# 192 of 512 tokens gather their expert rows instead of 128, and 64 of the dense tokens carry both weight parts in one stationary tile

## The chip, the cores and the metric

The kernel runs on one core of one Trainium2 chip. The metric is the device time of one execution in microseconds (us). The core has five engines: TensorE (PE in the profile, with its weight loads as PEld), VectorE (DVE), ScalarE (ACT), GpSimd (POOL) and SyncE (SP). 16 DMA engines move data; transfers are issued by SP, ACT and POOL.

## The reference, cut to what matters

One decoder layer over 512 tokens of width 1024. A mixing half (projections, a short convolution, a gated recurrence, an output projection) is followed by a feed-forward half that selects experts, and a last norm. The change touches the feed-forward half only:

```python
q = (xt @ wq).reshape(t, 8, 2, 128)                       # 8 heads, two halves
scores = einsum('thpd,hpnd->thpn', q, keys)               # 128 keys per half
s_top, i_top = lax.top_k(scores, 16)
cand = s_top[:, :, 0, :, None] + s_top[:, :, 1, None, :]  # 16 x 16 pairs
c_score, c_idx = lax.top_k(cand, 16)
expert = i1 * 128 + i2                                    # 1 of 16384
gates = softmax(c_score)
u = take(u_tab, expert); a = gelu(einsum('td,thkd->thk', x, u))
vv = take(v_tab, expert); y = einsum('thk,thkd->td', gates * a, vv)
```

So each token has 8 x 16 = 128 experts; an expert is one row of 1024 float32 (4096 bytes) in a table of u and one in a table of v.

## The kernel before, in words

**Two ways to the same sum.** Block 0 (tokens 0 to 127, one token a partition) gathers: for each of its 128 expert slots one indirect DMA of POOL brings a row of u per partition (`gu`, line 675), DVE multiplies it with the normed token and sums (line 677); later another brings the row of v (`gv`, line 683) and DVE adds it with its weight to `y0` (line 685). The other 384 tokens (`TD`) are dense: all 16384 experts are multiplied out, in 128 chunks of 128 experts, with the gates as a matrix that is zero where an expert wasn't chosen.

**Precision.** A dense product is made of three matmuls (`mm3`, lines 112 to 115): both factors are split in a high and a low part (`whi`, `wlo`, `wh`, `wl`), and high*high, low*high and high*low are added. ACT makes the high part (line 97), DVE the low one (line 99), for every 128x1024 tile of weights (`wraw`).

**Stages.**
- The mixing half, up to about 250 us.
- The query stage: 16 query projections (`query`), with the scores against the keys (`scores`, matmuls of line 535) and the 16 best of each half for four blocks of 128 tokens (`top16`: five DVE operations and more, lines 515 to 520).
- The gate stage: `pick` finds the 16 best pairs of each head, `lookup` their places, `gate_t` transposes them, and 24 calls of `gate_m` (16 tokens each) build the gate matrix: four DVE operations of 128x2048 (lines 641 to 644), 32 matmuls of float16 (lines 652, 653), four ACT copies, and after each second call a 2 MB write to `Gd` in HBM. Between these stand `uchunk`s: gelu(h2 U^T) of one chunk of 128 experts for the dense tokens, 24 matmuls with a moving side of 384 columns; its result `gl` goes to `Ad` in HBM for the first 84 chunks. 48 gather slots (`EARLY`) are also put here.
- The main loop: for each of 128 chunks `vchunk` loads v, multiplies `gl` with the gates (`Gt`, read back from `Gd`), splits the product `w` in `wh` and `wl`, and `vmm` adds into six PSUM banks: three blocks of tokens, two halves of the width, three matmuls each of 512 columns. In its first 41 rounds there is also a `uchunk`. `PACE` gives the gather slots taken in a round: 2.65 with a `uchunk`, 1.1 without; what is left is taken behind the loop.
- The end: the products of the last four chunks (`TAIL`), and `finish` of four blocks (residual, norm, output).

**What sets the order.** Every engine works through its own queue in order. The order in the queues is set when the program is built, by a scheduler that sorts the work of all engines by its own estimate of time. `wraw` tiles of loads and gathers share a ring: 8 in the gate stage, 12 (`MRING`) in the main loop; `whi` and `wlo` have four buffers each.

## Time and profile before

| what | value |
|---|---|
| median of three timed runs | 1545.05 us (1543.59 to 1545.79) |
| span of the profiled execution, first to last instruction | 1540.5 us |
| mean granted TensorE clock | 0.996 of full speed |
| busy of the span: PE, PEld, DVE, ACT, POOL | 99%, 87%, 79%, 41%, 24% |
| moved by DMA | 394.75 MB, 256 GB/s on average |
| chain that ended last | PE 93%, DMA 2%, DVE 2% |

The profiled execution has no other time than its span; the timed runs take 4.5 us more, which lie around the first and the last instruction. A share of the whole span is a mean over stages that have different limits; the stages are read from windows. An engine's busy time is the union of its instructions: where one starts before the other's record has ended, the step from start to start is what one costs.

### The profile page before, as it was taken

Reading aid. Unit: us, or ns where it says so; the run is one execution under the profiler, and the core shown is the slowest. Engines: PE = TensorE matmul, PEld = TensorE weight load, DVE = VectorE, ACT = ScalarE, POOL = GpSimd, SP = SyncE. Lnnn points to the kernel's source line nnn. Section 1 sums busy time; section 2 is a strip of 40 time slices with the busy share of each in tenths; the row PEclk is TensorE's granted clock in tenths of the full one; section 3 lists DMA queues with packets and bytes.
Section 4 is the critical chain, followed back from the end, with each engine's and each line's share of the span. In section 5 each row is a group of like instructions: output and inputs, shape, how many; then the busy total and the mean of one; then the engine's idle time right before and its main releaser. Section 6 shows DMA issues by size and latency. Waiting matters only on the chain.

```text
span 1540.5 us, 21785 instructions
## 1 busy us (share of the span) xinstructions
PE 1517.9 (99%) x7929; PEld 1337.1 (87%) x7929; DVE 1212.7 (79%) x2312; ACT 638.6 (41%) x900; POOL 368.8 (24%) x300
## 2 busy tenths in 40 slices
PE   7999999999999999999999999999999999999997
PEld 6887777889999999999999998989898888888886
DVE  5846875899999987876738787777888788878787
ACT  5833334333443456466643333333333333333333
POOL 0000000000053231322014444444343233333340
PEclk9999999999999999999999999999999999999999
DMA  6221234523479787788679998999999999999983
GB/s 231 86 92 56 82 112 162 187 83 117 163 251 373 264 251 252 242 271 269 209 236 412 354 333 303 330 336 326 329 326 364 340 342 353 340 347 346 327 313 138
DMA packets 164653, 394.75 MB, mean 256 GB/s; under 512 B 13249, under 2 KB 84417, under 8 KB 164417
## 3 DMA queue, kind: packets, MB, share of 16 engines
q1 hardware_dynamic: 47520, 170.94, 30.7%
q0 software_dynamic: 41472, 159.40, 28.7%
q10 hardware_dynamic: 75552, 63.01, 12.8%
q8 instruction: 62, 1.02, 0.3%
q14 instruction: 47, 0.38, 0.1%
HBM read 346.90 MB, written 46.40 MB: 255 GB/s over the span
## 4 chain that ended last, share of the span: by engine, by line
PE 93%; DMA 2%; DVE 2%; ACT 1%; issue 1%; POOL 0%; ACTq 0%; DVEq 0%; SPq 0%; POOLq 0%
PE y L113 12%; PE y L114 12%; PE y L115 12%; PE pa L115 10%; PE pa L113 10%; PE pa L114 10%; PE pm L113 6%; PE pm L115 6%; PE pm L114 6%; PE pm L652 3%; PE pm L653 3%; PE pm L535 1%; PE pm L299 1%; DMA wraw<-in_u_dram,e_i 1%; DVE wlo L99 1%; DMA wraw<-in_v_l_dram 1%
## 5 line engine op out<-in xcount | busy, mean ns | idle before, releaser
L97 ACT ACTIVATE whi<-wraw 128x1024 fp32r<-128x1024 f32 x308 | 325.8, 1058 | 514.2 <-PE pa L114 197.9
L99 DVE TENSOR_TENSOR wlo<-wraw,whi 128x1024 fp32r<-128x1024 f32 x308 | 377.1, 1224 | 160.7 <-ACT whi L97 158.5
L113 PE MATMUL pa<-h2Thi,whi 128*128 128x384 f32 x1024 | 345.3, 337 | 2.5 <-ACT gl L444 2.5
L115 PE MATMUL pa<-h2Thi,wlo 128*128 128x384 f32 x1024 | 344.9, 337 | 0.3 <-DVE wlo L99 0.3
L114 PE MATMUL pa<-h2Tlo,whi 128*128 128x384 f32 x1024 | 344.5, 336 | 0.0
L114 PE MATMUL y<-wlo,wh 128*128 128x512 f32 x768 | 304.3, 396 | 0.0
L115 PE MATMUL y<-whi,wl 128*128 128x512 f32 x768 | 304.0, 396 | 0.0
L113 PE MATMUL y<-whi,wh 128*128 128x512 f32 x768 | 303.7, 397 | 0.0
L671 POOL DMA_INDIRECT wraw<-in_u_dram,e_i x128 | 174.9, 1366 | 492.5 <-DMA Ad<-gl 178.5
L671 POOL DMA_INDIRECT wraw<-in_v_dram,e_i x128 | 171.8, 1342 | 301.1 <-DVE wlo L99 136.9
L113 PEld LDWEIGHTS pa<-h2Thi,whi 128*128 128x128 f32 x1024 | 192.8, 188 | 6.0 <-ACT gl L444 3.7
L114 PEld LDWEIGHTS pa<-h2Tlo,whi 128*128 128x128 f32 x1024 | 192.8, 188 | 1.8
L115 PEld LDWEIGHTS pa<-h2Thi,wlo 128*128 128x128 f32 x1024 | 192.7, 188 | 0.9 <-DVE wlo L99 0.6
L115 PEld LDWEIGHTS y<-whi,wl 128*128 128x128 f32 x768 | 144.7, 188 | 35.4
L685 DVE SCALAR_TENSOR_TENSOR y<-wraw,w,y 128x1024 f32<-128x1024 f32 x128 | 163.8, 1280 | 13.8 <-DMA wraw<-in_v_dram,e_i 13.7
L743 ACT ACTIVATE wh<-w 128x384 fp32r<-128x384 f32 x128 | 67.1, 524 | 258.6 <-PE y L114 199.0
L113 PEld LDWEIGHTS y<-whi,wh 128*128 128x128 f32 x768 | 144.6, 188 | 33.2
L114 PEld LDWEIGHTS y<-wlo,wh 128*128 128x128 f32 x768 | 144.5, 188 | 33.2
L677 DVE SCALAR_TENSOR_TENSOR wraw<-wraw,h2n 128x1024 f32<-128x1024 f32 x128 | 155.9, 1219 | 18.7 <-DMA wraw<-in_u_dram,e_i 18.7
L745 DVE TENSOR_TENSOR wl<-w,wh 128x384 fp32r<-128x384 f32 x128 | 71.1, 556 | 53.0 <-ACT wh L743 52.6
L655 ACT ACTIVATE stg<-pm 128x512 f32<-128x512 f32 x96 | 94.3, 1161 | 19.5 <-PE pm L653 19.1
L652 PE MATMUL pm<-B,A 128*128 128x128 f16 x384 | 91.1, 296 | 0.2 <-ACT stg L655 0.2
(242 smaller groups left out, 1817.7 us busy)
## 6 DMA issues: line engine op xcount, KB each, us to landing
wraw<-in_u_l_dram SPq DMA_DIRECT2D x128, 512.0 KB, 5.3
wraw<-in_v_l_dram SPq DMA_DIRECT2D x128, 512.0 KB, 6.5
Gd<-stg ACTq DMA_DIRECT2D x12, 2048.0 KB, 9.9
Gt<-Gd POOLq DMA_DIRECT2D x32, 768.0 KB, 8.2
Ad<-gl ACTq DMA_DIRECT2D x84, 192.0 KB, 4.5
glr<-Ad ACTq DMA_DIRECT2D x84, 192.0 KB, 5.9
wraw<-in_w_in_dram SPq DMA_DIRECT2D x24, 512.0 KB, 3.7
wraw<-in_wq_dram SPq DMA_DIRECT2D x16, 512.0 KB, 8.3
```

The costliest lines, as they stand in the source:

```text
L97: S.activation(hi, src, AF.Copy)
L99: V.tensor_sub(lo, src, hi.bitcast(F32))
L113: PE.matmul(out, l[0], r[0], start=first, stop=False)
L114: PE.matmul(out, l[0], r[1], start=False, stop=False)
L115: PE.matmul(out, l[1], r[0], start=False, stop=last)
L652: PE.matmul(o3[:, t, :], A[:, q, :, t], B2[:, q, :, t], start=True, stop=False)
L655: S.activation(st[:, t0:t0 + 4, :], o3, AF.Copy, scale=1.0 / GSC)
L671: G.indirect_dma_start(out=t, out_offset=None, in_=a[tab], in_offset=bass.IndirectOffsetOnAxis(ap=e_i32[:, j:j + 1], axis=0))
L677: V.scalar_tensor_tensor(r, r, 1.0, h2n, op0=OP.mult, op1=OP.mult, accum_out=act0[:, j:j + 1])
L685: V.scalar_tensor_tensor(y0, r, w0[:, j:j + 1], y0, op0=OP.mult, op1=OP.add)
L743: S.activation(wh, w, AF.Copy)
L745: V.tensor_sub(wl, w, wh.bitcast(F32))
```

## The change

- `TD` falls from 384 to 320. Block 0 gathers as before. Of block 1 the first 64 tokens gather too, each on two partitions (p and p + 64), which take 64 of its experts each: 64 further slots of `gu` and `gv`, with `h2n1` and `y01` in place of `h2n0` and `y00`. So there are 192 slots, 384 indirect DMAs.
- The dense tokens are 64 of block 1 and the blocks 2 and 3. `uchunk` has 320 moving columns. For the 64 tokens the stationary tile `wx[:, 0:128]` holds `wh` beside `wl`, so that two matmuls (with `vhi` and `vlo`) take the place of three; the sum of both halves is made at the end with a 0/1 matrix (`fold`), which also adds the two partitions of the gathered 64 tokens.
- `gate_m` is called 20 times, not 24.
- Selection: the query stage finishes the 16 best for blocks 0 and 1 only. The scores of blocks 2 and 3 are kept (`late`) and finished by `best_late` in the gate stage; `pick` works on two blocks at a time.
- `EARLY` goes from 48 to 110, `PACE` from (2.65, 1.1) to (2.9, 1.1).

```diff
-TD = T - P
+HALF = P // 2
+ND0 = P + HALF
+TD = T - ND0
+NG = ND0
-EARLY = 48
-PACE = (2.65, 1.1)
+EARLY = 110
+PACE = (2.9, 1.1)
...
-            mm3(o, (w[0][:, sl], w[1][:, sl]), (h2T[0][:, dc, P:], h2T[1][:, dc, P:]), dc == 0, dc == ND - 1)
+            mm3(o, (w[0][:, sl], w[1][:, sl]), (h2T[0][:, dc, ND0:], h2T[1][:, dc, ND0:]), dc == 0, dc == ND - 1)
...
-        s = s2.tile([P, NB, NK], F32, tag="B1", name="s")
-        S.activation(s.rearrange("p a b -> p (a b)"), o, AF.Copy)
-        for tb in (1, 2, 3, 0):
-            top16(s[:, tb, :], NK, topv[tb][:, i // 2, i % 2, :], topi[tb][:, i // 2, i % 2, :])
+        s = s2.tile([P, 2, NK], F32, tag="B1", name="s")
+        S.activation(s, o[:, 0:2, :], AF.Copy)
+        S.activation(late[:, i, :, :], o[:, 2:4, :], AF.Copy)
+        for tb in (0, 1):
+            best(tb, i, s[:, tb, :])
...
     slots = [(gu, j) for j in range(16)]
-    for b in range(1, 8):
+    for b in range(1, NG // 16):
         for j in range(16):
             slots += [(gu, 16 * b + j), (gv, 16 * b - 16 + j)]
-    slots += [(gv, 112 + j) for j in range(16)]
+    slots += [(gv, NG - 16 + j) for j in range(16)]
...
-    work = [(14.0, experts0, ()), (30.0, pick_dense, ())]
+    work = [(25.0, pick_two, (0,)), (11.0, experts0, ()), (13.0, gate_t, (1,))]
+    first = len(work)
+    work += [(3.5, best_late, (i,)) for i in range(NHP)] + [(25.0, pick_two, (2,))]
     for tb in (1, 2, 3):
-        work.append((8.0, gate_t, (tb,)))
-        for b in range(8):
-            work.append((4.6, gate_m, (tb, b)))
+        if tb > 1:
+            work.append((12.0, gate_t, (tb,)))
+        for b in range(4 if tb == 1 else 0, 8):
+            work.append((4.9, gate_m, (tb, b)))
...
-        wl = vp.tile([P, TD], F32R, tag="wl", name="wl", bufs=4)
-        V.tensor_sub(wl, w, wh.bitcast(F32))
+        wx = wp.tile([P, TD + HALF], F32R, tag="wx", name="wx")
+        S.activation(wx[:, 0:HALF], w[:, 0:HALF], AF.Copy)
+        V.tensor_sub(wx[:, HALF:], w, wh.bitcast(F32))
...
+            if k == 0:
+                PE.matmul(yp[0][hf], wx[:, 0:P], vh[:, cs], start=first, stop=False)
+                PE.matmul(yp[0][hf], wx[:, 0:P], vl[:, cs], start=False, stop=last)
+            else:
+                c = HALF + (k - 1) * P
+                mm3(yp[k][hf], (wh[:, c:c + P], wx[:, c + HALF:c + HALF + P]), (vh[:, cs], vl[:, cs]), first, last)
...
+                PE.matmul(o, fold[:, 0, :], y0[1][:, cs], start=True, stop=False)
+                PE.matmul(o, fold[:, 1, :], yh[:, cs], start=False, stop=True)
```

How the order moves is seen at two places of DVE's queue. The first is the selection. Before, in the query stage, the queue takes all four blocks of tokens (`tv_2182` to `tv_2185`) of one half of a head through:

```order
L515 MAX tv_2183<-s 128x8
L515 MAX tv_2184<-s 128x8
L515 MAX tv_2185<-s 128x8
L515 MAX tv_2182<-s 128x8
L516 MAX_INDEX ti_2187<-tv_2183,s 128x8
L518 MATCH_REPLACE mr<-tv_2183,s 128x128
L516 MAX_INDEX ti_2188<-tv_2184,s 128x8
L518 MATCH_REPLACE mr<-tv_2184,s 128x128
```

After the change, behind the last query and in front of the first gather, three of the five operations of the blocks 2 and 3 (`tv_2191`, `tv_2192`, out of `late`) stand between the rows of the first `lookup` (`oh`):

```order
L610 TENSOR_TENSOR oh<-pa,iota_2187 128x2048
L525 MATCH_REPLACE mr<-tv_2191,late 128x128
L525 MATCH_REPLACE mr<-tv_2192,late 128x128
L613 TENSOR_TENSOR oh<-oh,tif 128x2048
L526 MAX tv_2191<-mr 128x8
L526 MAX tv_2192<-mr 128x8
L614 TENSOR_TENSOR oh<-oh 128x128x8
L608 CAST tif<-ti_2194 128x128
L527 MAX_INDEX ti_2195<-tv_2191,mr 128x8
L527 MAX_INDEX ti_2196<-tv_2192,mr 128x8
```

All 32 such selections have moved behind the query stage with these three operations; the first two stayed in it. The second place is the end of the main loop. Before, one gather slot stands behind the last `wl` (line 745), and then the last norm (line 789):

```order
L99 TENSOR_TENSOR wlo<-wraw,whi 128x1024
L745 TENSOR_TENSOR wl<-w,wh 128x384
L685 SCALAR_TENSOR_TENSOR y_2161<-wraw,w_2159,y_2161 128x1024
L789 TENSOR_TENSOR wraw<-wraw,y_2161 128x512 x2
L792 TENSOR_TENSOR m_13907<-fms 128x1
```

After the change the last `wx` (line 778) is followed by gather slots of u (line 703) and v (line 712) up to the last norm (line 827). The first five rows and, after them, the last five:

```order
L778 TENSOR_TENSOR wx<-w,wh 128x320
L703 SCALAR_TENSOR_TENSOR wraw,act_2159<-wraw,h2n_2162 128x1024
L707 TENSOR_TENSOR w_2160<-w_2160,gate_2158 128x16
L712 SCALAR_TENSOR_TENSOR y_2164<-wraw,w_2160,y_2164 128x1024
L703 SCALAR_TENSOR_TENSOR wraw,act_2159<-wraw,h2n_2162 128x1024
```

```order
L712 SCALAR_TENSOR_TENSOR y_2164<-wraw,w_2160,y_2164 128x1024
L707 TENSOR_TENSOR w_2160<-w_2160,gate_2158 128x16
L712 SCALAR_TENSOR_TENSOR y_2164<-wraw,w_2160,y_2164 128x1024 x16
L827 TENSOR_TENSOR wraw<-wraw,y_2163 128x512 x2
L827 TENSOR_TENSOR wraw<-wraw,y_7931 128x512
```

Between them rows of lines 703 and 712 take turns: 49 gather slots in all (16 of u, 33 of v) now stand behind the last `wx`, where 1 stood. In front of the first `wx` stand 111 slots, where 49 stood in front of the first `wl`; 224 lie in the main loop between them, where 206 lay.

## Rows read from the trace of the kernel before

**Rows 1.** The page, parts 1 and 2: busy us of each engine, GB/s in 40 slices

```profile
PE 1517.9 (99%) x7929; PEld 1337.1 (87%) x7929; DVE 1212.7 (79%) x2312; ACT 638.6 (41%) x900; POOL 368.8 (24%) x300
GB/s 231 86 92 56 82 112 162 187 83 117 163 251 373 264 251 252 242 271 269 209 236 412 354 333 303 330 336 326 329 326 364 340 342 353 340 347 346 327 313 138
```

**Rows 2.** Windows (stretch, length; PE, PEld, DVE, ACT, POOL busy; PEclk, DMA share, GB/s)

```profile
369.00:450.00 81.00, 81.00 (x471) 80.88 (x470) 77.62 (x416) 37.74 (x49) 11.64 (x9) 1.00 0.53 178
450.00:550.00 100.00, 98.13 (x582) 96.34 (x581) 97.25 (x140) 41.81 (x57) 31.41 (x23) 1.00 0.87 309
369.00:778.00 409.00, 406.93 (x2567) 397.39 (x2566) 345.77 (x721) 210.12 (x263) 87.27 (x48) 1.00 0.76 251
800.00:850.00 50.00, 49.05 (x264) 46.26 (x263) 35.07 (x44) 18.12 (x27) 22.25 (x20) 1.00 1.03 405
821.00:1525.00 704.00, 704.00 (x3259) 599.74 (x3258) 571.08 (x735) 252.40 (x347) 269.27 (x230) 1.00 0.91 332
850.00:1150.00 300.00, 300.00 (x1500) 270.33 (x1499) 239.01 (x298) 108.44 (x147) 132.94 (x108) 1.00 0.91 330
1200.00:1500.00 300.00, 300.00 (x1282) 241.17 (x1281) 243.11 (x321) 105.87 (x146) 102.73 (x93) 1.00 0.94 340
```

**Rows 3.** The chain of waits (start us, us, what), its last row of line 535

```profile
368.70 0.89 PE pm L535 x8
```

**Rows 4.** Timeline (start us, us, engine, line, operation): four marks of DVE and PE

```profile
775.85 1.22 DVE L644 TENSOR_TENSOR B<-B,gt 128x2048 f16<-128x2048 f16 x1
...
821.07 0.39 PE L113 MATMUL y<-whi,wh 128*128 128x512 f32 x1
...
1518.63 0.55 DVE L745 TENSOR_TENSOR wl<-w,wh 128x384 fp32r<-128x384 f32 x1
...
1532.11 0.40 PE L115 MATMUL y<-whi,wl 128*128 128x512 f32 x1
```

**Rows 5.** Timeline of DVE around 1000 us

```profile
999.50 1.22 DVE L99 TENSOR_TENSOR wlo<-wraw,whi 128x1024 fp32r<-128x1024 f32 x1
1000.64 1.22 DVE L677 SCALAR_TENSOR_TENSOR wraw<-wraw,h2n 128x1024 f32<-128x1024 f32 x1
...
1001.78 1.29 DVE L685 SCALAR_TENSOR_TENSOR y<-wraw,w,y 128x1024 f32<-128x1024 f32 x1
1002.98 1.23 DVE L99 TENSOR_TENSOR wlo<-wraw,whi 128x1024 fp32r<-128x1024 f32 x1
```

**Rows 6.** Groups by line (count | busy us, mean ns | idle before)

```profile
L113 PEld LDWEIGHTS pa<-h2Thi,whi 128*128 128x128 f32 x1024 | 192.8, 188 | 6.0 <-ACT gl L444 3.7
...
L641 DVE TENSOR_TENSOR A<-iota,gt 128x2048 f16<-128x2048 f16 x24 | 29.3, 1222 | 14.9 <-PE pm L653 13.3 <-ACT gt L623 1.4
...
L520 DVE FIND_INDEX8 ti<-tv,mr 128x8 uint32<-128x128 f32 x64 | 18.0, 299 | 0.0
L518 DVE MATCH_REPLACE8 mr<-tv,s 128x128 f32<-128x128 f32 x64 | 17.8, 285 | 0.0
...
L535 PEld LDWEIGHTS pm<-keys,q 128*128 128x128 f32 x128 | 16.7, 191 | 1.3
L519 DVE MAX8 tv<-mr 128x8 f32<-128x128 f32 x64 | 15.5, 290 | 0.0
```

**Rows 7.** Timeline of POOL, indirect DMAs

```profile
548.24 8.10 POOL L671 DMA_INDIRECT wraw<-in_u_dram,e_i  x1 [13.48 <-DVE wlo L99]
...
808.38 0.94 POOL L671 DMA_INDIRECT wraw<-in_u_dram,e_i  x1 [0.30 <-issue]
809.62 0.94 POOL L671 DMA_INDIRECT wraw<-in_v_dram,e_i  x1 [0.30 <-issue]
```

**Rows 8.** The page, part 6 (count, KB each, us to landing)

```profile
Gt<-Gd POOLq DMA_DIRECT2D x32, 768.0 KB, 8.2
...
glr<-Ad ACTq DMA_DIRECT2D x84, 192.0 KB, 5.9
```

More of the change, by code (lines that the diff above doesn't have):

```diff
@@ L604, in lookup, with pick_two @@
         return idx[0], idx[1], gs[j]
[L606 to L618 removed]
+    gt = {}
+    picked = {}
+    def pick_two(a):
+        p = pick((a, a + 1))
+        for j in range(2):
+            picked[a + j] = (j, p)
+    def experts0():
+        i1, i2, g = lookup(0, *picked[0])
+        V.scalar_tensor_tensor(e_i32[:, 0:P], i1, float(NK), i2, op0=OP.mult, op1=OP.add)
+        V.tensor_copy(gate0[:, 0:P], g)
+    def gate_t(tb):
+        i1, i2, g = lookup(tb, *picked[tb])
+        if tb == 1:
+            e = sp.tile([P, P], I32, name="e1")
+            V.scalar_tensor_tensor(e, i1, float(NK), i2, op0=OP.mult, op1=OP.add)
+            for i in range(2):
+                hs, cs = slice(i * HALF, (i + 1) * HALF), slice(i * HALF, (i + 1) * HALF)
+                nc.sync.dma_start(out=e_i32[hs, P:NG], in_=e[0:HALF, cs])
+                nc.sync.dma_start(out=gate0[hs, P:NG], in_=g[0:HALF, cs])
         o = ps()
@@ L712, in body @@
             nu += 1
-        while f is gate_m and ng < EARLY * done / total:
+        while ng < EARLY * (done - head) / (total - head):
             take(1)
@@ L802, in body @@
         nc.sync.dma_start(out=xs[tb], in_=x1d[tb])
-    finish(0, [y0[:, 0:T], y0[:, T:]])
-    for tb in range(3):
+    fold = vp.tile([P, 2, P], F32, name="fold", bufs=1)
+    S.dma_start(out=fold, in_=a["fold"])
+    finish(0, [y0[0][:, 0:T], y0[0][:, T:]])
+    yh = ring[0]()
+    for hf in range(2):
+        for n, ops in enumerate(tail):
+            vmm(ops, 0, False, n == TAIL - 1, (hf,))
+        S.activation(yh[:, hf * T:(hf + 1) * T], yp[0][hf], AF.Copy)
+    for k in (1, 2):
         for hf in range(2):
             for n, ops in enumerate(tail):
-                vmm(ops, tb, False, n == TAIL - 1, (hf,))
-        finish(tb + 1, yp[tb])
+                vmm(ops, k, False, n == TAIL - 1, (hf,))
+        if k == 1:
+            yf = []
+            for hf in range(2):
+                cs = slice(hf * T, (hf + 1) * T)
+                o = psA.tile([P, T], F32, tag="a", name="pf")
+                PE.matmul(o, fold[:, 0, :], y0[1][:, cs], start=True, stop=False)
+                PE.matmul(o, fold[:, 1, :], yh[:, cs], start=False, stop=True)
+                yf.append(o)
+            finish(1, yf)
+        finish(k + 1, yp[k])
 def kernel(x, norm_mix, w_in, conv_w, conv_gain, hg_lb_logits, hg_gain, w_out, norm_ffn, peer_wq, peer_keys,
```

63 lines of the change are left out of this document (34 added, 29 removed).

## The prediction

> **What bounds the kernel now.** I read the engines' busy times first, then windows stage by stage, then the chain of waits and single rows for prices. PE is busy 99% of the span [rows 1], so the whole looks like a PE kernel. The windows say more [rows 2]. In the main loop (821:1525) PE is busy 704.0 of 704 us, DVE 571.1 (81%), and DMA moves 332 GB/s at a share of 0.91: PE sets the pace, but the other two have only a fifth to spare. In the stage before it (369:778) PE is busy 406.9 of 409 us, yet DVE 345.8 (85%), and in its first part DVE is the fuller one: 77.6 of 81 us and 97.25 of 100. The reader is to see that the change takes work from PE and gives work to DVE and DMA, in stages where DVE is close behind PE. So each stage has to be asked again which engine ends last.
>
> The timed runs take 4.55 us more than the profiled span of 1540.5; I work in the span and add 4.55 at the end.
>
> **Prices.** With 42 matmuls in a chunk of the main loop's first part, 1500 matmuls in 300 us make 8.40 us a chunk; with 18 in the second part 1282 make 4.21 us [rows 2]. So a matmul of 512 columns costs 0.234 us and one of 384 costs (8.40 - 4.21) / 24 = 0.1745 us. One of 320 columns is not in the trace. In proportion to columns it is 0.1455, by the slope between the two known ones 0.1446, and if nothing is gained 0.1745. I take 0.146, the row of 384 scaled, and keep 0.1745 as the other end.
>
> On DVE the steps from start to start are 1.14 us for a `wlo`, 1.14 for the product with a row of u (reading the sum out included) and 1.20 for adding a row of v [rows 5]: 1.17 a gather slot on average. A DVE operation of `gate_m` is 29.3 / 24 = 1.22 us. The three late operations of a selection are (17.8 + 15.5 + 18.0) / 64 = 0.80 us, with the overlap of their records some 0.75 [rows 6].
>
> On TensorE a weight load could be the limit of a shorter matmul. In the rows, loads of 128 columns are 188 ns long, longer than the 174.5 ns from one 384-column matmul to the next, and PEld is busy 397.4 of 409 us [rows 2, 6]. But the score matmuls of 128 columns have a load of their own each, of 191 ns, and eight of them take 0.89 us, 111 ns each [rows 3, 6]. So a load's record is longer than what it holds up, and 146 ns are to be had. The Trainium skill (Perfetto Trace Analysis, Identifying the Most-Contended Engine) calls the busy share of LDWEIGHTS a good measure of how near PE is to its limit. By that rule, 97% here, the narrower matmul would gain nothing; the score rows speak against it, and it is a rival below.
>
> **The stage from the last scores to the main loop.** Before, the last scores are at 368.7, the last DVE operation of a `gate_m` starts at 775.9, and the first main-loop matmul at 821.1 [rows 3, 4]. PE's own work in this stage falls: some 80 chunks by 24 x 28.5 ns = 55 us, and 128 float16 matmuls. DVE's rises. To the 345.8 us busy before [rows 2] come
> - 62 more gather slots (111 in front of the first `wx`, 49 before): 62 x 1.17 = +72.5;
> - 16 operations of four `gate_m` less: 16 x 1.22 = -19.5;
> - 32 selections with three operations each, moved here: 32 x 0.75 = +24. In the query stage, where PE sets the pace, they cost nothing and their leaving gains nothing.
>
> Together 423 us. PE needs less than 409 - 55 = 354 us, so DVE sets the pace. DVE doesn't run without gaps: in the two windows in which it is fullest it is busy 95.8% and 97.25% [rows 2]. I take 95%, as POOL must bring in 111 slots through a ring of 8, and an indirect DMA was once held up for 8.10 us there [rows 7]. 423 / 0.95 = 445 us. It begins some 3 us earlier than before, at 366 (four narrower chunks lie in the query stage), so DVE's last gate and gather work is at 811. Behind it stand eight chunks of u for PE, 8 x 24 x 0.146 = 28 us, and 2 us of splitting: the main loop begins at 841 and not at 821. **+20 us**, with ends of -2 (DVE busy 100%) and +56 (88%).
>
> Where DVE stands behind PE now, PE waits in front of each `wlo`: what is queued behind it there are the gate matmuls, for which ACT's copies wait, and nothing else.
>
> **The main loop.** Before: from 821.1 to the end of the last matmul at 1532.5 [rows 4], 711.4 us. After: a chunk of v has 16 matmuls of 512, 3.75 us, and 40 rounds have 24 matmuls of 320 besides: 128 x 3.75 + 40 x 3.50 = 620, with 3 us for the folded halves and joints 623. **-88 us.** With 0.1745 for the narrower matmul it is -61.
>
> Does the rest follow? DVE has in a round with a `uchunk` 2 x 1.14 + 2 x 0.42 + 2.9 x 1.17 = 6.5 us of 7.25 (`w` and `wx` from 384 to 320 columns, 0.48 us less a sixth), and without 1.14 + 0.84 + 1.1 x 1.17 = 3.3 of 3.75. It follows, at 88 to 90%. DMA: before, 704 us at 332 GB/s are 234 MB [rows 2]. After come 224 - 206 = 18 slots of 0.524 MB (+9.4), and `Gt` (32 of 768 KB) and `glr` (84 of 192 KB) shrink by a sixth (-4.2, -2.7) [rows 8]: 236 MB in the 611 us up to the last slot of the loop, 387 GB/s. The most that a window of 50 us shows is 405 GB/s, at a share of 1.03 [rows 2]. So DMA must run at 95% of the best it has shown, with the 12 `wraw` tiles in turn for 16 us each and not 19. In the 704 us before PE never waited at 332 GB/s. I take 15 us of waiting, **+15**, from 0 (405 GB/s are held) to +41 (652 us at 362 GB/s, which is what the second part of the loop moves, 340 at a share of 0.94, at a share of 1).
>
> The Trainium skill (DMA: Bandwidth & Descriptors, Where 436 GB/s comes from) holds that transfers between HBM and the core are bound by about 358 GB/s per core. By it the loop would take 236 / 0.358 = 659 us, 48 longer than 611. The window with 405 GB/s disagrees, for 50 us; whether such a rate lasts for 600 us no row here shows.
>
> **The end.** Before, one slot stands behind the last `wl` (1518.6); the span ends 8 us behind the last matmul. After, 49 slots stand behind the last `wx`. That `wx` can't be early: its `whi` and `wlo` take the buffers of four chunks before, so it comes about 13 us before PE's last product (1518.6 against 1532.5 [rows 4]). Then DVE needs 49 x 1.17 = 57 us; POOL issues one slot every 1.24 us where nothing holds it [rows 7], with some ten landed already; DMA at 405 GB/s brings one in 1.29 us. I take 60 us. PE is done after 13 of them and stands still. Then six additions in the queue, the fold (some 4 matmuls of float32), its two additions and the norm: 16 us, where 8 lie behind PE before. -13 + 60 + 16 - 8 = **+55 us**, from +48 to +68 (1.5 us a slot). The cover that hid these slots in the loop, PE's own matmuls, is gone here.
>
> **Sum.** +20 - 88 + 15 + 55 = +2: a span of 1542.5, a time of 1547 us. What PE saves in the loop goes back in two other places.
>
> **Rivals.**
> - *DVE and DMA keep up* (faster). The stage before the loop runs at 97.25%, as the fullest window does: 435 us, +10. The loop waits for nothing (0), the end costs +55. Sum -23: 1522 us. For it: in 450:550 DVE ran so at a DMA share of 0.87. Against: the stage then moves 128 MB (103 before, +32 for the slots, -7 for the sixth of `Gd` and `Ad`) in 435 us, 295 GB/s where 251 were moved, with the 512-byte rows of `Gd` in between.
> - *DMA sets the pace of the loop* (slower). One mechanism: DMA doesn't go beyond 362 GB/s, 236 MB take 652 us and not 611, and PE waits in front of each `wlo`, +41 in place of +15: 1573 us. It decides from 387 GB/s downwards. For it: share 0.91 to 0.94 in the loop already. Against: the window with 405.
> - *A 320-column matmul takes as long as one of 384* (the rule on weight loads): +27 in the loop and +5 in the eight chunks before it, DMA then has time (0 in place of +15): 1564 us.
> - *The gathers choke the gate stage* (the change then doesn't do what it says: the early slots don't hide there). If each of the 10 writes of `Gd` holds up an indirect DMA for 8 us and DVE stands behind it for half of that, +40: 1587 us.
>
> **How the numbers follow.** The forecast has 0.45, with a range of its own from 1533 to 1565 (DVE busy 96 to 94%, 5 to 28 us of waiting in the loop). Keeping up has 0.28, DMA 0.16, the weight loads 0.05, the choke 0.06. From 1520 to 1588 leaves out some 0.1 above (the worse halves of DMA and choke, and two prices together) and 0.1 below (DVE busy 98% and more, with a shorter end). About 0.2%, 3 us, is what a measurement of this kernel can tell: faster is below 1542, slower above 1548. The forecast's own range lies for 0.28 below, 0.19 within, and the rest above. Faster: 0.28 + 0.45 x 0.28 = 0.41. Same: 0.45 x 0.19 = 0.09. Slower: the rest, 0.50.
>
> **What would show it.** After: between the last scores and the first `y` matmul PE has gaps in front of `wlo`, DVE 93 to 97% busy, and the first `y` matmul is at 830 to 855 (right) or before 822 (wrong: DVE was not the bound). In the loop 3.75 us a chunk in the second part and 7.25 in the first show the price of 320 columns; more, with PE waiting for `wlo` and that for a DMA, shows the second rival. In the end PE stands still for some 45 us beside rows of lines 703 and 712; if the gap is under 30 us, the term of the end is wrong. The prediction as a whole is wrong if the time is below 1520: then the terms don't add up in a row but overlap.

## The result, and the profile after

The changed kernel takes **1635.07 us** (median of 4 runs, 1629.24 to 1636.16) beside 1545.31 us of the kernel before: a ratio of **1.0575**, 95% interval 1.0557 to 1.0593. It is slower by 90 us; forecast were 1547, with 1588 as the end of the range. The profiled execution has a span of 1632.7 us, 92.2 more than before. By the marks of the timeline (us from the span's start; the end is counted from the end of the last `y` matmul):

| stretch | before | predicted | after |
|---|---|---|---|
| start to first `y` matmul | 821.1 | 841 (+20) | 882.2 (+61) |
| first `y` to end of last `y` matmul | 711.4 | 638 (-73) | 667.3 (-44) |
| from there to the end of the span | 8.0 | 63 (+55) | 83.2 (+75) |

All three terms have the forecast sign, and all three are worse than forecast, by 41, 29 and 20 us. The page after, parts 1 and 2, beside [rows 1]:

```profile
PE 1410.0 (86%) x7553; PEld 1220.2 (75%) x7553; DVE 1324.2 (81%) x2493; ACT 627.9 (38%) x1034; POOL 548.8 (34%) x429
GB/s 218 91 78 73 84 116 256 87 84 106 64 335 383 230 336 266 316 302 299 310 290 349 394 344 376 377 356 378 363 379 399 369 329 354 342 351 325 311 359 223
```

PE is busy 108 us less and DVE 111 more. But no engine is near 99% any more. Windows of the changed kernel (columns as in [rows 2]):

```profile
369.00:450.00 81.00, 58.41 (x394) 57.63 (x393) 81.00 (x430) 26.87 (x39) 5.43 (x3) 0.88 0.28 88
366.00:835.28 469.28, 377.14 (x2493) 360.25 (x2491) 418.74 (x959) 196.64 (x255) 179.52 (x111) 0.90 0.79 270
450.00:850.00 400.00, 328.17 (x2157) 311.59 (x2156) 341.18 (x535) 174.04 (x221) 174.09 (x108) 0.90 0.90 309
882.00:1547.00 665.00, 630.44 (x3001) 527.81 (x3000) 571.35 (x768) 253.99 (x466) 311.84 (x257) 0.99 0.97 360
1547.00:1611.00 64.00, 2.52 (x11) 1.69 (x9) 54.66 (x60) 0.22 (x1) 43.35 (x38) 0.55 0.97 361
```

In the gate stage (450 to 850) PE is busy 82%, DVE 85%, and DMA has a share of 0.90: no engine is full, and each waits for others in turn. From 366, where the prediction lets VectorE's stretch begin, to the end of its last gate operation at 835.28 DVE is busy 418.7 of 469.3 us, 89%. In the loop DMA has a share of 0.97 at 360 GB/s. In the last stretch PE stands still for 61 of 64 us, and DMA has 0.97 again.

The marks, from the timeline of PE and DVE, with the last 320-column matmuls in front of the first `y` (they answer to [rows 4]):

```profile
881.80 0.31 PE L116 MATMUL pa<-h2Thi,whi 128*128 128x320 f32 x1
881.95 0.31 PE L117 MATMUL pa<-h2Tlo,whi 128*128 128x320 f32 x1
882.09 0.31 PE L118 MATMUL pa<-h2Thi,wlo 128*128 128x320 f32 x1
882.24 0.39 PE L787 MATMUL y<-whi,wx 128*128 128x512 f32 x1
...
1542.24 0.52 DVE L778 TENSOR_TENSOR wx<-w,wh 128x320 fp32r<-128x320 f32 x1
...
1548.43 1.10 PE L118 MATMUL y<-whi,wx 128*128 128x512 f32 x4
...
1612.71 3.78 PE L858 MATMUL pf<-y,fold 128*128 128x512 f32 x4 [63.18 <-DVE y L712]
```

The step from one 320-column matmul to the next is 0.147 us. PE waits 63.18 us in front of `fold` for the last gathered row.

What PE waited for in the gate stage, what VectorE waited for longest, and what ScalarE waited for there (waits from 400 to 882: us, times, longest); before, PE's waits in the same stage were 3 us in all:

```profile
PE pa L118 <- DVE wlo L102: 34.5, 13, 20.2
PE pa L116 <- ACT whi L100: 32.0, 13, 7.5
PE pa L116 <- ACT gl L447: 18.4, 8, 5.8
DVE wlo L102 <- ACT whi L100: 50.2, 16, 9.3
```

```profile
ACT gl L447 <- issue: 47.7, 6, 10.4
ACT whi L100 <- DMA wraw<-in_u_l_dram: 38.2, 15, 8.5
ACT whi L100 <- issue: 26.1, 4, 12.0
```

Half of what PE waits is for ACT (`whi` and `gl`), VectorE waits 50.2 us for ACT's `whi`, and ACT, apart from its waits for PE itself, waits longest for "issue" (47.7 + 26.1 us): for nothing but its own queue. The timeline of ACT (rows with ACTq are transfers that it issues) shows on what:

```profile
660.64 0.38 ACTq L684 DMA_DIRECT2D Gd<-stg  x1
661.07 0.44 ACT L447 ACTIVATE gl<-pa 128x320 f32<-128x320 f32 x1 [0.45 <-PE pa L118]
661.40 1.05 ACT L100 ACTIVATE whi<-wraw 128x1024 fp32r<-128x1024 f32 x1
661.53 11.14 ACTq L449 DMA_DIRECT2D Ad<-gl  x1
672.72 0.44 ACT L447 ACTIVATE gl<-pa 128x320 f32<-128x320 f32 x1 [10.27 <-issue]
```

The 2 MB write to `Gd` (4096 rows of 512 bytes) is issued in 0.38 us, but the next transfer on ACT's queue, the small write of `gl`, takes 11.14 us to issue, and ACT can do nothing else meanwhile. There are 9 such issues of 3.4 to 11.8 us, 80 us in all. Before there were 12 of 2.9 to 8.0 us, 55 us in all, and PE had enough in hand to pass over them.

Where PE has stood still, the clock that it is granted is lower too. It waits 5.84 us in front of 612.57, and then:

```profile
612.50:617.00 4.50, 4.40 (x15) 4.00 (x16) 4.50 (x8) 0.45 (x2) 0.00 (x0) 0.50 0.90 274
```

The granted clock is 0.50 there, the lower of its two levels (1.2 and 2.4 GHz), and the step from one 320-column matmul to the next about 0.27 us in place of 0.147. Up to the first `y` some 150 steps are as long as that, 18 us more for PE; before, the clock was 1.00 in this stage [rows 2].

### The profile page after: what moved, and what is told of

It reads as the page before. It is cut to its first block, busy times and chain, and to the rows that moved or that the text cites. A ratio compares the mean times of both kernels' runs of the same rounds, so it can differ in the third digit from the quotient of the medians.

```text
span 1632.7 us, 21621 instructions
## 1 busy us (share of the span) xinstructions
PE 1410.0 (86%) x7553; PEld 1220.2 (75%) x7553; DVE 1324.2 (81%) x2493; ACT 627.9 (38%) x1034; POOL 548.8 (34%) x429
## 5 line engine op out<-in xcount | busy, mean ns | idle before, releaser
L697 POOL DMA_INDIRECT wraw<-in_u_dram,e_i x192 | 261.9, 1364 | 445.6 <-DVE e_i L632 181.2
L116 PE MATMUL pa<-h2Thi,whi 128*128 128x320 f32 x1024 | 330.8, 323 | 50.5 <-ACT whi L100 32.0
L118 PE MATMUL pa<-h2Thi,wlo 128*128 128x320 f32 x1024 | 328.1, 322 | 44.1 <-DVE wlo L102 41.1
L697 POOL DMA_INDIRECT wraw<-in_v_dram,e_i x192 | 264.0, 1375 | 297.2 <-DVE wlo L102 115.7
L117 PE MATMUL pa<-h2Tlo,whi 128*128 128x320 f32 x1024 | 326.5, 319 | 0.0
L116 PE MATMUL y<-whi,wh 128*128 128x512 f32 x512 | 183.1, 402 | 26.0 <-ACT wh L775 26.0
L117 PE MATMUL y<-wlo,wh 128*128 128x512 f32 x512 | 204.9, 400 | 0.0
L118 PE MATMUL y<-whi,wx 128*128 128x512 f32 x512 | 182.1, 396 | 0.0
L118 PEld LDWEIGHTS y<-whi,wx 128*128 128x128 f32 x512 | 96.6, 189 | 23.6
L787 PE MATMUL y<-whi,wx 128*128 128x512 f32 x256 | 94.4, 401 | 1.9 <-ACT whi L100 1.8
L788 PE MATMUL y<-wlo,wx 128*128 128x512 f32 x256 | 94.0, 400 | 0.0
```

What stands on the lines that cost most here:

```text
L116: PE.matmul(out, l[0], r[0], start=first, stop=False)
L117: PE.matmul(out, l[0], r[1], start=False, stop=False)
L118: PE.matmul(out, l[1], r[0], start=False, stop=last)
L697: G.indirect_dma_start(out=t, out_offset=None, in_=a[tab], in_offset=bass.IndirectOffsetOnAxis(ap=e_i32[:, j:j + 1], axis=0))
L787: PE.matmul(yp[0][hf], wx[:, 0:P], vh[:, cs], start=first, stop=False)
L788: PE.matmul(yp[0][hf], wx[:, 0:P], vl[:, cs], start=False, stop=last)
```

## The experiments

All are edits of the changed kernel, unless said otherwise; times in us, the ratio is to the kernel before with its 95% interval. "Slots" is the time from the first `y` to the end of the last gather slot.

| run | time | ratio | first `y` | slots |
|---|---|---|---|---|
| changed kernel | 1635.1 | 1.0575 [1.0557, 1.0593] | 882.2 | 730 |
| e1_pieces | 1640.9 | 1.0622 [1.0581, 1.0663] | 879.6 | 740 |
| e2_glr8 | 1636.4 | 1.0575 [1.0536, 1.0614] | 889.2 | 728 |
| e3_pace | 1603.0 | 1.0376 [1.0336, 1.0415] | 880.8 | 704 |
| e4_sel | 1615.4 | 1.0446 [1.0411, 1.0482] | 862.8 | 735 |
| e5_halfv | 1613.6 | 1.0438 [1.0401, 1.0475] | 893.6 | 707 |
| e6_halfdve | 1623.9 | 1.0524 [1.0477, 1.0571] | 873.7 | 728 |
| e7_few | 1497.4 | 0.9701 [0.9659, 0.9743] | 812.3 | - |
| e8_three | 1585.4 | 1.0270 [1.0228, 1.0311] | 863.4 | 698 |
| e9_ring6 | 1663.3 | 1.0776 [1.0755, 1.0797] | 911.4 | 731 |
| e10_ring10 | 1670.3 | 1.0809 [1.0764, 1.0854] | 909.3 | 740 |
| e11_four | 1601.7 | 1.0378 [1.0358, 1.0398] | 869.4 | 710 |
| e12_tworings | 1619.4 | 1.0477 [1.0455, 1.0499] | 866.0 | 735 |
| e13_wide | 1601.7 | 1.0370 [1.0344, 1.0395] | 847.6 | 732 |
| e14_program_order | 1731.4 | 1.1221 [1.1185, 1.1258] | 873.5 | 833 |
| e15_before_wide (before) | 1543.0 | 0.9990 [0.9980, 1.0000] | 823.0 | - |
| e16_wide_three | 1553.6 | 1.0067 [1.0037, 1.0097] | 832.5 | 699 |
| e17_wide_three_rings | 1585.4 | 1.0253 [1.0223, 1.0282] | 862.0 | 702 |
| e18_mring16 | 1549.1 | 1.0020 [1.0004, 1.0035] | 830.9 | 692 |

One caution for all of them: the scheduler sorts the queues anew for each kernel, so an edit also moves instructions that it doesn't name. And first `y` and slots are read from the one execution that was profiled; that of e5, for one, took 7.6 us more than the median of its runs.

### The whole: what the added slots cost

**e7_few**: only the 256 transfers of the first 128 slots.

```diff
+    slots = [s for s in slots if s[1] < P]
-EARLY = 110
-PACE = (2.9, 1.1)
+EARLY = 48
+PACE = (2.65, 1.1)
```

> The changed kernel without the 128 gather slots of the 64 added tokens, with 48 slots in front of the loop and 2.65 and 1.1 a chunk in it as before: what TensorE saves, and no added gathers. The added tokens' experts are left out of the output. By the prediction's terms (stage with DVE at 95 percent about as long as before less 10 us, loop 623 to 640, end as before plus 8) the first y matmul is at 790 to 815 and the time 1430 to 1460. The difference to 1635 is then the price of 128 slots, 175 to 205 us, 1.4 to 1.6 us each (0.524 MB at 330 to 385 GB/s), more than the 1.17 us that VectorE needs. If the narrower matmuls or the folded halves gained little, the time is over 1500.

Measured 1497.4: TensorE's part alone gains 46.6 us (1544.0 for the kernel before in the same run), less than the 85 to 115 expected. The first `y` (812.3) was in its range; the loop was not: from 1200 to 1400 PE is busy 179 of 200 us and does 736 matmuls, 4.35 us a chunk of 16 where 3.75 had been expected, at 342 GB/s. The products `w` stand in clumps of four there, as in e2's account below; e2's edit wasn't tried on this kernel, so how much that costs stays open. The 128 further transfers then cost 137.6 us, 1.08 each, and turn the gain over.

### The stage before the loop

**e4_sel**: all four blocks selected in the query stage, as before.

```diff
-        for tb in (0, 1):
+        for tb in (0, 1, 2, 3):
             best(tb, i, s[:, tb, :])
-    work += [(3.5, best_late, (i,)) for i in range(NHP)] + [(25.0, pick_two, (2,))]
+    work += [(25.0, pick_two, (2,))]
```

> The changed kernel, but the sixteen best of all four token blocks are selected in the query stage, as before. Theory G: VectorE's 24 us of moved selections set the end of the stage before the loop: first y matmul at 855 to 865 instead of 882, time 1610 to 1620. Rival H: that stage waits for DMA and for ScalarE more than for VectorE's work: first y matmul within 6 us of 882 and the time within 6 us of 1635.

First `y` 19.4 us earlier, time 19.7 less: theory G. The 24 us of VectorE cost most of their length. It shows from 369 to 450: the changed kernel has DVE 81 of 81 us busy and PE 58.4 (above); here PE is busy 81 of 81:

```profile
369.00:450.00 81.00, 81.00 (x556) 81.00 (x555) 81.00 (x420) 41.30 (x56) 2.39 (x1) 1.00 0.51 162
```

**e6_halfdve** and **e5_halfv**: half of VectorE's work on the slots, and half of the bytes of v's rows.

```diff
-        V.scalar_tensor_tensor(y, r, w0[:, j:j + 1], y, op0=OP.mult, op1=OP.add)
+        V.scalar_tensor_tensor(y[:, 0:T], r[:, 0:T], w0[:, j:j + 1], y[:, 0:T], op0=OP.mult, op1=OP.add)
```

```diff
-        r = rows("v", j)
+        r = ring[0]()
+        G.indirect_dma_start(out=r[:, 0:T], out_offset=None, in_=a["v"].rearrange("e (h d) -> (e h) d", h=2), ...
```

> The changed kernel, but VectorE works on only half of each gathered row (512 of 1024 numbers): 384 operations of about 0.6 us instead of 1.17, 219 us of VectorE less (63 of them in front of the loop), with all transfers as they were. The output is not that of the reference. Theory F (DMA is the bound): the loop keeps 7.3 to 7.4 and 4.0 to 4.1 us a chunk, the idle end keeps 60 us or more, first y within 10 us of 882; time 1620 to 1635. Theory J (VectorE is the bound): first y 40 to 60 us earlier, end under 40 us, time under 1560.

> The changed kernel, but each gathered row of v is only half a row (512 of 1024 numbers, used twice): 192 slots move 0.262 MB instead of 0.524, 50 MB less, with VectorE's, PE's and POOL's instructions as they were. The output is not that of the reference. Theory F (DMA is the bound from the first gather on; loop and end ran at share 0.97 to 0.99): the first y matmul comes 15 to 30 us earlier, the first part of the loop falls from 7.4 to 7.25 us a chunk and the second towards 3.8, the idle end from 64 to some 54 us; time 1570 to 1590. Theory J (VectorE or POOL's issue is the bound): the end keeps its 64 us, first y within 6 us of 882, time 1625 to 1637.

Neither frees the stage: -8.5 us and +11.4. Windows of 550 to 650 and 650 to 750, of e6 and then of e5:

```profile
550.00:650.00 100.00, 81.43 (x564) 76.77 (x563) 77.67 (x103) 48.52 (x61) 36.53 (x29) 0.87 0.95 326
650.00:750.00 100.00, 85.78 (x561) 80.65 (x560) 68.58 (x83) 48.60 (x60) 27.88 (x22) 0.86 0.89 296
```

```profile
550.00:650.00 100.00, 72.05 (x475) 67.78 (x473) 80.02 (x93) 38.75 (x50) 52.75 (x26) 0.88 0.75 254
650.00:750.00 100.00, 84.74 (x560) 80.47 (x561) 86.86 (x97) 42.74 (x52) 55.26 (x27) 0.90 0.78 256
```

With DVE down to 69 to 78% the stage is hardly shorter, and with DMA down to 0.75 it is longer. So neither alone is the bound; for this stage F's first `y` and time came in e6 and not in e5, J's in neither. But e6 isn't VectorE's work alone: in the order made for it VectorE's last gate operation starts at 771.9, 62 us earlier, with 19 chunks of u behind it and not 10, and its held issues are 30 us, not 80.

**e1_pieces**: each write of `Gd` in four, meant to take ACT's standing away.

```diff
+            for k in range(4):
+                parts.append((blk, stg[0], slice(8 * k, 8 * k + 8)))
```

> The changed kernel, but each of the ten writes of Gd (2 MB in rows of 512 bytes) is issued in four pieces, one behind each of the next four chunks of u. Theory A: the stage before the main loop is long because ScalarE stands still in front of the Ad write that follows a Gd write (nine times 3.4 to 11.8 us, 80 us in all, where before it was eleven times 2.9 to 8 us). Then no Ad issue takes over 3 us, the first y matmul comes 30 to 50 us earlier (832 to 852, not 882), and the time falls to some 1595 us. Rival B: the stage is bound by what DMA can move beside the 512-byte rows (share 0.85 to 0.97 there). Then the wait goes elsewhere, the first y matmul stays within 8 us of 882 and the time within 8 us of 1635.

No change of the first `y` (879.6), as theory B had it. But this isn't a test of A: the scheduler put the four pieces side by side, and ACT stood at these. Its timeline:

```profile
687.30 9.00 ACTq L660 DMA_DIRECT2D Gd<-stg  x4
696.41 0.44 ACT L447 ACTIVATE gl<-pa 128x320 f32<-128x320 f32 x1 [9.13 <-issue]
```

Over the stage 66 us of such issues (of more than 1 us each) were left of 80. What bears on A and B is the waits in e13.

**e9_ring6** and **e10_ring10**: the ring of `wraw` in this stage with 6 and 10 tiles.

```diff
-    raw_ring(sel.enter_context(tc.tile_pool(name="rs", bufs=1)), 8)
+    raw_ring(sel.enter_context(tc.tile_pool(name="rs", bufs=1)), 6)
```

> The changed kernel with 6 instead of 8 wraw tiles in the stage before the loop. Theory R: this stage is bound neither by VectorE's time nor by bytes (halving either on the gathers moved its end by 8 us or less) but by the ring: 111 gathers and 79 chunks of u pass through 8 tiles in turn, 190 tiles in 432 us, so each tile is held for 18 us, and a gather of u or v takes a place from a chunk of u. With 6 tiles and the same 18 us the stretch takes up to 576 us; as a tile is held for less when fewer transfers run at once I expect half of that rise: the first y matmul at 930 to 1000, the time 1680 to 1750. Rival S (the instructions' order couples PE, ScalarE and VectorE, the ring has room): first y at 877 to 900, time under 1655.

> The changed kernel with 10 instead of 8 wraw tiles in the stage before the loop (room from three constants that live in the front's pool, and from oh, which takes a buffer of A). Theory R: the stretch from 450 to 882 falls towards 432 x 8 / 10 = 346 us, as far as TensorE's own work there allows: first y at 820 to 850, time 1585 to 1605. Rival S: first y within 10 us of 882, time 1625 to 1640.

With 6 tiles +29 us, with 10 tiles +27: neither R's numbers nor S's came. That the number of tiles holds the stage (R) is not borne out. e10 is no clean test of it, as `oh` shares a buffer with the gate operations' `A` there, in front of which VectorE waits 18.4 us (2.8 in the changed kernel). **e11_four** (e8 below, with 10 tiles in the same way) says no more for R, 869.4 where e8 has 863.4.

> The kernel with the three edits (selections in the query stage, 3.2 and 1.5 slots, 8 glr buffers) and 10 wraw tiles in the stage before the loop. Theory R: first y at 815 to 840 (863 without), the loop bound by DMA as there, 697 us to the last slot; time 1535 to 1560, about that of the kernel before. Rival S: 1578 to 1590.

Then three runs to part what was left. **e12_tworings**: 4 tiles for chunks of u and 4 for gathers.

```diff
-        t = ring[0]()
+        t = gring[0]()
```

> The changed kernel with two rings of 4 tiles in the stage before the loop, one for chunks of u and one for gathers, instead of one ring of 8 for both. Theory K (loads of u wait on SyncE's queue for VectorE to finish gathers in front of them in the ring, 183 us of SyncE's waits in 450 to 850): loads come in time, TensorE's waits for whi (32 us) go, first y at 840 to 865, time 1590 to 1618. Theories L and M: first y at 870 to 910, time 1623 to 1665.

**e13_wide**: `Gd` laid out by token blocks, so that a write has 128 rows of 16 KB, and the small rows are in the loads of `Gt`.

```diff
-    Gd = dr.tile([NK // 4, P, TD // CH, 4, CH], F32, name="Gd")
+    Gd = dr.tile([TD // CH, P, NK // 4, 4, CH], F32, name="Gd")
...
-            S.dma_start(out=Gd[:, :, blk].rearrange("g p c t -> p g (c t)"),
-                        in_=stg[0].rearrange("p g c t -> p g (c t)"))
+            S.dma_start(out=Gd[blk].rearrange("p g c t -> p (g c t)"),
+                        in_=stg[0].rearrange("p g c t -> p (g c t)"))
```

> The changed kernel with Gd laid out by token blocks: each of its ten writes is 128 rows of 16 KB instead of 4096 rows of 512 bytes, and the small rows move to the loads of Gt in the main loop. Theory L: no Ad issue holds ScalarE over 3 us, no load of u is late, first y at 830 to 860; the loop gets longer by the 41 thousand small rows there, by 20 to 60 us. Theories K and M: first y at 872 to 905.

**e14_program_order**: no sorting by estimated times.

```diff
-    with tile.TileContext(nc, schedule_with_timeline_sim=True) as tc, ...
+    with tile.TileContext(nc, schedule_with_timeline_sim=False) as tc, ...
```

> The changed kernel with the instructions of each engine in the order in which the program writes them, not in the order that a timing model makes of it. Theory M (the order made for a machine with quicker transfers is what the stage loses on): first y outside 870 to 910. I expect it later, 920 to 1000, as the program's order is coarse (16 selections or eight gate operations in a row in front of the next wlo), and TensorE's waits in front of wlo in the stage over 120 us. Theories K and L: the order matters little, first y at 870 to 910.

e13 is the one that counts: first `y` at 847.6, **-34.6 us**, time -33. Theory L. VectorE is busy 95.5% up to its last gate operation, which ends at 803:

```profile
366.00:802.80 436.80, 370.61 (x2482) 355.75 (x2481) 416.97 (x959) 196.59 (x252) 189.65 (x111) 0.91 0.79 289
```

The price that was given for it did not come: the loop is as long as before (732 beside 730). In ACT's timeline no write holds the next one any more, and in its waits "issue" is gone, while the wait for loads of u is no smaller (50.3 us, 38.2 in the changed kernel). VectorE waits 18.9 us for `whi`, where it waited 50.2. So what went is ACT's standing, not late loads:

```profile
671.76 0.33 ACTq L684 DMA_DIRECT2D Gd<-stg  x1
674.46 0.44 ACT L447 ACTIVATE gl<-pa 128x320 f32<-128x320 f32 x1 [2.72 <-PE pa L118]
674.93 0.33 ACTq L449 DMA_DIRECT2D Ad<-gl  x1
```

```profile
ACT gl L447 <- PE pa L118: 136.9, 49, 26.7
ACT whi L100 <- DMA wraw<-in_u_l_dram: 50.3, 21, 7.8
ACT whi L100 <- PE pa L117: 18.8, 10, 2.1
DVE wlo L102 <- ACT whi L100: 18.9, 6, 12.1
```

The Trainium skill (Perfetto Trace Analysis, Optimizing DMA Performance, What "DMA-bound" means) counts the sequencer that issues a transfer as a bound of its own, beside the DMA engines, and names large descriptors as the cure for both. The 11.14 us row and e13 agree.

e12 gives -16 us, a little outside K's range, and leaves 26 of the 80 us of held issues, so it isn't a clean test of the ring. It can also turn round: **e17** (below) has two rings and is 29 us later than the same kernel with one. The loads of u run ahead there, PE waits 38 us for VectorE's gate operations, and then stands for 63.5 us in one piece:

```profile
854.90 0.64 PE L116 MATMUL pa<-h2Thi,whi 128*128 128x320 f32 x1 [63.51 <-ACT whi L100]
```

The load of that chunk is issued only at 850.13, just behind VectorE's last gathered row of the stage. In e12 PE stands for 23.8 us at the same place. That the ring of the main loop waits there for the room of the two may be the reason; no run tests it.

e14 ends the stage at 873.5, as with the sorted order, so M's sign did not come, and my 920 to 1000 missed; it costs 100 us in the loop instead. That a second order loses as much doesn't show that none loses less.

**e15_before_wide**: the same layout in the kernel before.

> The kernel before with Gd laid out by token blocks, its writes in rows of 16 KB. There the Ad issue holds ScalarE too (12 times, 55 us), but TensorE waits 3 us in all in that stage. Theory L (the rows cost time where no engine has slack left, so here nothing is to be gained as TensorE sets the pace): time within 3 us of 1545. If the rows cost TensorE time by themselves: 1525 to 1540.

1543.0, ratio 0.999 [0.998, 1.000]: the held issues are gone there too, and nothing measurable is gained. There PE always has work in hand; in the changed kernel it hasn't.

### The loop and the end

**e3_pace**: a pace for 47 slots more in the loop; 42 more land there, and 7 stand behind the last `wx` in place of 49.

```diff
-PACE = (2.9, 1.1)
+PACE = (3.2, 1.5)
```

> The changed kernel with 3.2 and 1.5 gather slots a chunk instead of 2.9 and 1.1: 47 slots more in the main loop and hardly any behind the last wx. Theory E: the loop has room for them (VectorE busy 80 to 88 percent): PE's idle stretch at the end falls from 64 to under 10 us, the loop grows by under 10 us, and the time falls to some 1575 to 1585 us. Rival F: DMA is the bound of the loop as of the end (45 slots took 64 us, 368 GB/s): the 47 slots then cost 24.6 MB / 0.365 = 67 us wherever they stand, and the time stays within 10 us of 1635.

PE's idle end goes and the loop gets 36 us longer: 704 us in place of 730 to the last slot, time -32, between the two theories. Windows of e3:

```profile
1200.00:1500.00 300.00, 260.38 (x1052) 203.75 (x1051) 258.63 (x360) 106.89 (x201) 153.12 (x122) 0.96 0.99 378
880.00:1585.00 705.00, 643.00 (x3015) 534.87 (x3013) 625.11 (x830) 257.54 (x471) 361.97 (x295) 0.98 0.98 373
```

705 us at 373 GB/s are 263 MB. Now DMA is full from the first `y` to the last slot, and further slots cost their bytes. In the kernel as changed the second part of the loop left some room (next run) that was paid for at the end.

**e2_glr8**: 8 buffers for `gl` read back.

```diff
-            gl = vp.tile([P, TD], F32, tag="glr", name="glr", bufs=4)
+            gl = vp.tile([P, TD], F32, tag="glr", name="glr", bufs=8)
```

> The changed kernel with 8 buffers instead of 4 for the gelu values read back (glr), so that VectorE's products w come one by one and not in clumps of four. Theory C: the second part of the loop takes 4.1 us a chunk, not 3.75, because PE waits 14 times for the first wh of a clump (26 us). Then these waits go, the second part takes 3.8 to 3.9 us a chunk and the time falls by 15 to 25 us, to 1610 to 1620. Rival D: DMA sets the pace there (share 0.93 to 1.0 at 334 to 350 GB/s). Then a chunk still takes 4.05 to 4.15 us, PE waits for wlo instead, and the time stays within 6 us of 1635.

In the changed kernel the scheduler had put the products `w` in clumps of four, and PE waited for the first `wh` of each; these are most of its waits in the loop (882 to 1550):

```profile
PE y L116 <- ACT wh L775: 26.0, 14, 3.4
PE pa L118 <- DVE wlo L102: 6.6, 6, 2.1
```

Windows of 1200 to 1500, the changed kernel and e2:

```profile
1200.00:1500.00 300.00, 274.37 (x1143) 215.75 (x1141) 245.38 (x343) 114.56 (x213) 120.72 (x100) 0.99 0.97 356
```

```profile
1200.00:1500.00 300.00, 283.63 (x1199) 224.54 (x1198) 255.44 (x353) 120.19 (x228) 117.96 (x101) 1.00 0.97 359
```

The waits for `wh` go, a chunk of 16 matmuls takes 4.0 us in place of 4.2, and the loop falls to 651 us. But DMA moves hardly more (359 beside 356 GB/s), 62 slots and not 49 are left behind the last `wx`, and the time is the same: a wait taken away in front of a full DMA. C was right on the waits, D on the time.

**e5_halfv** belongs here too: with 0.26 MB less in every second slot the first part of the loop is at PE's pace (1349 matmuls in 250 us, 40 a chunk, 7.4 us; 1325 in the changed kernel) and PE is busy 98% in the second. The end, though, gets no quicker: 45 slots take 72 us behind PE's last product, and with VectorE halved (e6) 38 take 55; 43 take 63 in the changed kernel. So neither v's bytes nor VectorE alone paces it. POOL's timeline in the changed kernel, which answers to [rows 7]:

```profile
531.03 15.54 POOL L697 DMA_INDIRECT wraw<-in_v_dram,e_i  x1 [14.92 <-DMA wraw<-in_u_l_dram]
...
1547.54 1.97 POOL L697 DMA_INDIRECT wraw<-in_v_dram,e_i  x1 [0.30 <-issue]
1549.81 0.94 POOL L697 DMA_INDIRECT wraw<-in_u_dram,e_i  x1 [0.30 <-issue]
1551.06 0.94 POOL L697 DMA_INDIRECT wraw<-in_v_dram,e_i  x1 [0.30 <-issue]
...
1600.69 0.94 POOL L697 DMA_INDIRECT wraw<-in_v_dram,e_i  x1 [0.30 <-issue]
```

It issues without a break from 1547.54 to 1600.69: 36 steps, 1.48 us each, 1.24 where nothing holds an issue and up to 2.3 where one is held, with DMA at a share of 0.97. With halved v rows (e5) the steps are 1.41 at a DMA share of 0.65, and VectorE still has 19 us of rows to add when POOL is done. My reading, which no run tests by itself: issue, transfers and VectorE lie so close together here (1.2 to 1.5 us a slot) that relieving one hands the end to the next.

### All together

**e8_three** is e4, e3 and e2 in one; **e16** is that with e13's layout; **e17** has two rings besides; **e18** is e16 with `MRING = 16`.

> The changed kernel with three edits together: all selections in the query stage, 3.2 and 1.5 slots a chunk, 8 buffers for glr. The first two gave -19 and -31 us each; the third took the clumps away without a gain, since slots moved to the end. Theory F (DMA at 375 to 380 GB/s bounds everything from the first y matmul on, 266 MB, 700 us): first y at 860 to 865, last slot at 1560 to 1565, time 1580 to 1588. If the clumps were a loss of their own, 1565 to 1575.

> The changed kernel with Gd in rows of 16 KB, all selections in the query stage, 3.2 and 1.5 slots a chunk and 8 glr buffers. If the parts add: first y at 863 - 35 = 828, 697 us more to the last slot as DMA is full there (380 GB/s), then 20 us: time 1547 to 1553, no faster than the kernel before. If they overlap in the stage: first y at 840 to 850, time 1558 to 1572.

> The same with two rings of 4 tiles in the stage. If the ring's 16 us come on top: first y at 812 to 820, time 1530 to 1540, a little faster than the kernel before. If VectorE is then the bound of the stage (346 + 72.5 - 19.5 = 399 us from 366 on, at 95 percent 420): first y at 815 to 835, time 1533 to 1555.

> The kernel with Gd in rows of 16 KB, all selections in the query stage, 3.2 and 1.5 slots a chunk, 8 glr buffers, and 16 instead of 12 wraw tiles in the main loop. Theory F (the DMA engines are full there, about 266 MB at 380 GB/s): first y to last slot 692 to 702 us as with 12 tiles, time 1547 to 1557. Theory N (the ring of 12 holds the loop, a tile 16 us): 660 to 685 us, time 1515 to 1540, faster than the kernel before.

The parts add up: 1585.4 with three, 1553.6 with the layout too. Windows of e16, and of e18:

```profile
550.00:650.00 100.00, 89.96 (x606) 84.74 (x605) 98.40 (x110) 47.42 (x61) 52.01 (x29) 0.93 0.93 343
900.00:1150.00 250.00, 240.92 (x1284) 213.46 (x1284) 227.86 (x296) 97.51 (x170) 143.04 (x114) 0.99 1.00 380
```

```profile
900.00:1150.00 250.00, 245.38 (x1315) 216.03 (x1315) 233.99 (x303) 98.87 (x175) 155.76 (x116) 1.00 1.02 392
```

In e16 the stage is what was forecast for it, VectorE's (98.4 of 100 us here, 96% from 366 to its last gate operation), and the loop is DMA's. Four more tiles give 392 GB/s here, 375 in place of 373 from the first `y` to the last slot, and 7 us: theory F, with a little of N. So the best version with the change stands at 1549.1 beside 1545.2 (ratio 1.0020 [1.0004, 1.0035]): level with the kernel before, and no version with the change that does the whole computation beats it.

## Why the prediction was wrong

**The prices were right.** 0.146 us for a 320-column matmul; measured 0.147, so weight loads were no limit, though their records are 197 ns long ([rows 6] has 188):

```profile
L116 PEld LDWEIGHTS pa<-h2Thi,whi 128*128 128x128 f32 x1024 | 201.7, 197 | 59.5 <-ACT whi L100 36.1
```

The rule of the Trainium skill that the prediction weighed (Perfetto Trace Analysis, Identifying the Most-Contended Engine), by which the busy share of weight loads tells how near PE is to its limit, doesn't hold for this kernel: PEld was at 97% in the stage before [rows 2], and the narrower matmul still took its share of columns. Slots are where they were counted, 111 before the loop and 49 behind the last `wx`. The transfers shrank as in the sum (answering to [rows 8]):

```profile
Gt<-Gd POOLq DMA_DIRECT2D x32, 640.0 KB
...
glr<-Ad ACTq DMA_DIRECT2D x84, 160.0 KB
```

**The stage, +61 for +20.** VectorE's work was counted right: 418.7 us up to its last gate operation, with 423 forecast. The step that failed is "I take 95%": it was busy 89%, and that operation ended at 835 and not 811 (+24). A second term was too small, the 30 us "behind it": 47 us passed from there to the first `y` (+17), with ten chunks of u and not eight; [rows 4] have 44 us there before the change. And the sentence that behind a waiting `wlo` stand the gate matmuls "and nothing else" left out ACT's queue.

e13 shows what lay behind the 95%: with the writes of `Gd` in long rows VectorE is busy 95.5%, its last gate operation ends at 803, and the first `y` comes at 847.6, within the 830 to 855 given. So 35 of the 41 us missed go with the short rows. That they cost the time through ACT's standing is read from the waits, of ACT, VectorE and PE, that go in e13; no run takes the standing away and leaves the rows. e6 and e12 lost more than half of the held issues and gained 8 and 16 us, but each moved other queues too. The rival on these writes had the right culprit and size and a wrong route: it held up POOL's gathers, at 40 us and a chance of 0.06, and stood as an alternative to the forecast. In the changed kernel one gather of the stage is held for more than 4 us, the one of 15.54, and it stands in front of the first write of `Gd` (572.47) and in e13 too. The rows on ACT were there before: twelve issues of `Ad`, 55 us, on a queue that isn't counted as busy; PE's backlog covered them and I didn't ask what they cost without it.

The selections were sized right (+24, measured 19). The prices took PE's clock as full; it was granted 0.90 on average in the stage, 18 us of longer steps, of which 15 stay in e13. How much of that lies on the path, and what else makes up the 45 us that stay behind VectorE's last gate operation in e13, is open: the engines wait for each other in turn, and an edit to one moves the queues of all.

**The loop, -44 for -73.** PE was busy 633 of its 667 us, 10 more than forecast, and waited 34. The step that failed is the choice of +15 us of waiting between 0 and +41 by a window of 50 us at 405 GB/s. Such a rate was not held: the most over 250 us was 396 GB/s (e18) and 394 (e3). The rival "DMA sets the pace of the loop" came for loop and end together: without the clumps the time is the same (e2), and in e3 and e16 the engines are full at 373 GB/s. That its number fits the loop alone (362 GB/s assumed, 360 moved over 665 us; -88 + 41 = -47) is partly luck. Its sign was PE waiting in front of `wlo`, and that was 6.6 us; 26 were in front of the first `wh` of a clump, which nothing in the prediction names. With 373 GB/s its 236 MB take 633 us, +22. The Trainium skill (DMA: Bandwidth & Descriptors, Where 436 GB/s comes from) puts transfers between HBM and one core at about 358 GB/s, by which the loop would have taken 659 us, an estimate. The changed kernel's 360 GB/s agree to 1%, while e3, e16 and e18 show that it is no firm limit.

**The end, +75 for +55.** The 49 slots took 70.5 us, 1.44 each, where 1.22 had been taken from POOL's best step; the range's 1.5 was the better row. The last `wx` came 7 us before PE's end, not 13, and what follows the slots takes 20 us, not 16: PE, idle from 1549.5 on, is granted a clock of 0.55 on average from 1547 to 1611 (0.50, the lower level, from 1555 on), and the four products with `fold` behind that take 3.78 us; how much of the 20 us this makes, no run shows.

**The sum.** Of the four rivals the one on DMA came for loop and end, the one on the writes of `Gd` in its size, and both at once. 1547 + 41 + 29 + 20 = 1637; the 2 us beyond the measured time are the surplus of the timed runs over the span, taken at 4.55 us and here 2.4. In one and the same execution it is 1.8 us (1634.47 and 1632.7 here, 1544.28 and 1542.5 in e15), so not all of the 4.5 lies around the first and the last instruction. Terms that lie in three stretches in a row don't exclude each other; the range, to 1588, had room for about one of them.

## What to carry to other kernels

Taking work from an engine that is 99% busy and giving it to two that are 80 to 90% busy removes the backlog that hid every small wait, so price those first: go through the issue rows of each compute engine's queue for transfers that stand behind a write of many small rows, and lay such a tensor out with long rows. Count the bytes of the whole stretch against a rate that was held for as long, not against the best 50 us. And where rivals lie in different stretches, add them before setting the range.
